# Setting the planned durations of TensorE's and GpSimd's work in a kernel that orders its own instructions

## The chip, the cores and the metric

The kernel runs on one core of a Trainium2 chip. The metric is the device time of one execution in microseconds; lower is better. PE is TensorE, DVE is VectorE, ACT is ScalarE, POOL is GpSimd, and SP is the engine whose queue issues all DMAs here.

## The reference

A decoder trunk of two layers on one sequence of 256 tokens with 1024 features, in float32. Each layer is a token mixer and an MLP, each followed by a LayerNorm of `ALPHA * x + f(x)`:

```python
for i in range(DEPTH):                      # DEPTH = 2
    if i % 2 == 0:
        mix = moba_attention(h, ...)        # 16 heads of 64; one block of 256, so causal attention
    else:
        mix = dilated_attention(h, ...)     # 12 heads: windows (128, 1), (512, 4), (2048, 16)
    h = layer_norm(ALPHA * h + mix, ...)
    h = layer_norm(ALPHA * h + square(relu(h @ w_in)) @ w_out, ...)   # 1024 -> 4096 -> 1024
```

Queries and keys get a rotary embedding. In the second mixer the outputs of the three head groups are weighted by their softmax denominators, which comes to one softmax over the keys of all three groups.

## The kernel before

**Arithmetic.** Each float32 matrix is split into a high and a low part of a shorter format (`split`, L281): ACT writes the high part as a rounded copy, DVE subtracts it from the source for the low part. A product is then three matmuls: high by high, high by low, low by high. A tile of weights is 128 x 1024 (512 KB); it is loaded into one of 4 buffers `raw` and split into `whi` and `wlo`, of which there are 10 each. A `raw` buffer comes free when both splits have read it, a `whi` and `wlo` when PE has used them.

**Steps of PE.** `mm_wstat` (L400) multiplies one tile of weights, held stationary, by all 256 tokens, in eight steps over the features. The narrow form (queries and keys) has three matmuls of 256 columns for a step; the wide form (the MLP's first matrix) has one of 512 and one of 256. `mm_xstat` (L419) holds the tokens stationary; it makes the values ("V steps", n columns each) and the first 512 columns of each MLP. `mm_rows` (L434) adds one tile of a second matrix into the accumulators `acc`, three matmuls for each piece of up to 512 columns ("row steps"). `score` (L500), `transposes` (L534) and `weigh` (L548) are the attention.

**Attention.** For each pair of heads: queries and keys are projected; `rotate` (L464) does three DVE multiplications out of PSUM and one addition on POOL (`ADD_ENG`), and splits the result into `qhi`, `qlo`, `khi`, `klo`, the keys once for each head of the pair. Then come the scores (in PSUM buffers `tp`, of which there are 4), on DVE the mask with the row maximum (`mx`, L515), on ACT the exponentials (L525), on DVE the scaling of `sc` (L532), on PE the transposes, on ACT the copy `pt` to SBUF (L545), and on PE the weighing of the values. Layer 0 has eight such pairs, layer 1 six.

**LayerNorm** (`ln_half`, L618): statistics on DVE, `rstd` as a power on POOL (L638), two DVE steps for each 512 columns, and, but for the last one, transposes and splits into `xs`, the stationary or moving operand of what follows. It is done for the two halves of 128 tokens (m = 0, 1). Behind it the first 512 columns of an MLP go through `hrt` (L699, L700).

**The order of instructions** isn't that of the program text. Each piece of work is given to `plan.op(engine, cost, function, reads, writes)`; `cost` is a planned duration in microseconds, written by hand. `Plan.order` (L112) then simulates the engines with these costs and issues the functions in the order of the planned starts. First a pass in program order gives each PE step a due time, and each other piece the latest time that its users allow:

```python
t = max([clock.get(o.eng, 0.0)] + [p.end + p.lat for p in o.preds])
...
d = q.due - o.cost - o.lat
o.due = d if o.due is None else min(o.due, d)
```

Then a list scheduler takes, engine by engine, the piece that can start first, and of several that can, the one with the earliest due time. A piece can start when its operands are ready (their end plus `LAT` = 0.15 us, none from PE to PE), its engine is free, and its buffers are free. DVE alone may wait for a more urgent piece (`PATIENT`). DMAs keep their program order; a load is planned at 360 GB/s plus 2.1 us. On the chip each engine takes its instructions in the planned order and waits with semaphores for what isn't ready, so whatever stands behind a waiting instruction on that engine waits too. The program order in attention is written out by hand (`ORDER0`, `ORDER1`, L33 to L35).

The planned costs of DVE and ACT are formulas in the number of columns n (L272 to L276): `n / 960 + 0.07` for an ordinary DVE instruction, `n / 1200 + 0.055` for ACT from PSUM and `n / 1200 + 0.093` from SBUF, with additions for scalar operands.

Of the kernel before, what the change touches and what calls it, by code (L numbers as in the profile page):

```python
# [10 lines left out]
ALU = mybir.AluOpType  # L11

P = 128
S = 256
# [49 lines left out]
class Plan:  # L64
# [16 lines left out]
    def op(self, eng, cost, fn, reads=(), writes=(), lat=LAT, early=0.0):  # L81
        o = Op()
        o.n, o.eng, o.cost, o.fn, o.lat = len(self.ops), eng, cost, fn, lat
        o.early = early
        o.preds, o.succs, o.bufs = set(), [], set()
        for group, is_write in ((reads, False), (writes, True)):
            for item in group:
                b, key = item if isinstance(item, tuple) else (item, None)
                o.bufs.add(b)
                for k, st in b.state.items():  # L90
                    if key is None or k is None or k == key:
                        if st[0] is not None:
                            o.preds.add(st[0])
                        if is_write:
                            o.preds.update(st[1])
                st = b.state.setdefault(key, [None, []])
                if is_write:
                    if key is None:
                        b.state = {None: [o, []]}
                    else:  # L100
                        st[0], st[1] = o, []
                else:
                    st[1].append(o)
        o.preds.discard(o)
        for p in o.preds:
            p.succs.append(o)
        for b in o.bufs:
            b.left += 1
        self.ops.append(o)
        return o  # L110
# [112 lines left out]
def tile_trunk(  # L223
# [23 lines left out]
    nc = tc.nc  # L247
    plan = Plan()
    op = plan.op
# [12 lines left out]
    def mk(shape, dt, tag, bufs, space=None):  # L262
        uid[0] += 1
        return plan.buf(Bufs(space or sb, bufs), shape, dt, tag, bufs, f"{tag}_{uid[0]}")
# [80 lines left out]
    expo = mk([P, 1], F32, "expo", 1)  # L345
# [51 lines left out]
    def xk(kt, ms):  # L397
        return [(xs[kt // 4], (part, kt, m)) for part in range(2) for m in ms]

    def mm_wstat(ps, w, kts=range(KT), wide=False):  # L400
        for kt in kts:

            def go(kt=kt):
                c = slice(kt * P, (kt + 1) * P)
                a, b = (xs[kt // 4].t[:, kt % 4, part, :] for part in range(2))
                first, last = kt == 0, kt == KT - 1
                if wide:
                    both = xs[kt // 4].t[:, kt % 4, :, :].rearrange("p h s -> p (h s)")
                    mm(ps.t, w.hi.t[:, c], both, first, False)
                    mm(ps.t[:, S:], w.lo.t[:, c], a, False, last)  # L410
                else:
                    mm(ps.t[:, :S], w.hi.t[:, c], a, first, False)
                    mm(ps.t[:, :S], w.hi.t[:, c], b, False, False)
                    mm(ps.t[:, :S], w.lo.t[:, c], a, False, last)

            i = wkey(w, kt * P)
            op("PE", 0.327, go, [(w.hi, i), (w.lo, i)] + xk(kt, (0, 1)), [ps])

    def mm_xstat(ps, ws, m, n):  # L419
        t = slice(m * P, (m + 1) * P)  # L420
        for kt in range(KT):
            per = 1024 // n
            w = ws[kt // per]

            def go(kt=kt, w=w):
                c = slice((kt % per) * n, (kt % per + 1) * n)
                a, b = (xs[kt // 4].t[:, kt % 4, part, t] for part in range(2))
                mm(ps.t[:, :n], a, w.hi.t[:, c], kt == 0, False)
                mm(ps.t[:, :n], a, w.lo.t[:, c], False, False)
                mm(ps.t[:, :n], b, w.hi.t[:, c], False, kt == KT - 1)  # L430

            op("PE", 3 * (n / 2400 + 0.003), go, [(w.hi, 0), (w.lo, 0)] + xk(kt, (m,)), [ps])

    def mm_rows(pieces, item, m):  # L434
        (ahi, alo, j), w, pos, total = item
        first, last = pos == 0, pos == total - 1
        t = slice(m * P, (m + 1) * P)

        def go():
            a, b = ahi.t[:, j, t], alo.t[:, j, t]  # L440
            for acc, c0, n in pieces:
                mm(acc.t[:, :n], a, w.hi.t[:, c0 : c0 + n], first, False)
                mm(acc.t[:, :n], a, w.lo.t[:, c0 : c0 + n], False, False)
            for acc, c0, n in pieces:
                mm(acc.t[:, :n], b, w.hi.t[:, c0 : c0 + n], False, last)

        op(
            "PE", 3 * sum(n / 2400 + 0.003 for _, _, n in pieces), go,
            [(w.hi, 0), (w.lo, 0), (ahi, (j, m)), (alo, (j, m))], [acc for acc, _, _ in pieces],
        )  # L450

    def tt(n, out_ap, a, b, alu, r, w, eng="DVE"):
        if eng == "DVE":
            op("DVE", dve(n), lambda: nc.vector.tensor_tensor(out_ap(), a(), b(), op=alu), r, w)  # L454
        else:
            op("POOL", n / 480 + 0.1, lambda: nc.gpsimd.tensor_tensor(out_ap(), a(), b(), op=alu), r, w)  # L456

    def stt(n, aps, dst, a, s, b, o0, o1, r, w):
        op(
# [40 lines left out]
    def score(ps, q, k, qc, kc, off=0):  # L500
        (qhi, qlo), (khi, klo) = q, k
        n = kc.stop - kc.start

        def go():
            o = ps.t[:, off : off + 2 * n].rearrange("p (h s) -> p h s", h=2)
            mm(o, qhi.t[:, qc], khi.t[:, :, kc], True, False)
            mm(o, qhi.t[:, qc], klo.t[:, :, kc], False, False)
            mm(o, qlo.t[:, qc], khi.t[:, :, kc], False, True)

        op("PE", 3 * (2 * n / 2400 + 0.003), go, [qhi, qlo, khi, klo], [ps])  # L510

    def mask_min(n, dst, src, mask, init, accum, r, w):
        op(
# [34 lines left out]
    def weigh(o, v, vc, pt, n, c0, start, stop):  # L548
        def go():
            for h in range(2):  # L550
                c = slice(vc + 64 * h, vc + 64 * h + 64)
                mm(o.t[64 * h : 64 * h + 64, c0 : c0 + n], v.t[:, c], pt(h), start, stop)

        return go
# [10 lines left out]
    def pv_causal(p0, p1, r0, r1, v, vc, ahi, alo, j):  # L565
        t0, t1 = psum("tp"), psum("tp")
        transposes(
            t0,
            [(h * S, p0[h]) for h in range(2)] + [(h * S + P, lambda h=h: p1[h]()[:, 0:P]) for h in range(2)],
            r0 + r1,  # L570
        )
        transposes(t1, [(h * P, lambda h=h: p1[h]()[:, P:S]) for h in range(2)], r1)
        pt0, pt1 = copy_out(512, t0, "pt0"), copy_out(S, t1, "pt1")
        o = psum("tp")
        op("PE", 0.482, weigh(o, v[0], vc, lambda h: pt0.t[:, h * S : (h + 1) * S], S, 0, True, False),
           [v[0], pt0], [o])
        op("PE", 0.27, weigh(o, v[1], vc, lambda h: pt1.t[:, h * P : (h + 1) * P], P, P, False, True),
           [v[1], pt1], [o])
        attn_out(o, ahi, alo, j, True)

    def pv_full(e, c0, r, v, vc, ahi, alo, j):
        pts = []
        for kb in range(2):
            t = psum("tp")
            transposes(
                t, [(h * S + m * P, lambda h=h, m=m, kb=kb: e[m][h].t[:, c0 + kb * P : c0 + (kb + 1) * P])
                    for h in range(2) for m in range(2)], r,
            )
            pts.append(copy_out(512, t, f"pt{kb}"))
        o = psum("tp")  # L590
        for kb in range(2):
            op("PE", 0.482,
               weigh(o, v[kb], vc, lambda h, kb=kb: pts[kb].t[:, h * S : (h + 1) * S], S, 0, kb == 0, kb == 1),
               [v[kb], pts[kb]], [o])
        attn_out(o, ahi, alo, j, False)

    def pv_diag(e, c0, r, v, vc, ahi, alo, j):
        t = psum("tp")
        transposes(
            t, [(h * S + m * P, lambda h=h, m=m: e[m][h].t[:, c0 : c0 + P]) for h in range(2) for m in range(2)], r  # L600
        )
        pt = copy_out(512, t, "pt0")
        o = psum("tp")
        for m in range(2):
            op("PE", 0.27,
               weigh(o, v[m], vc, lambda h, m=m: pt.t[:, h * S + m * P : h * S + (m + 1) * P], P, m * P, True, True),
               [v[m], pt], [o])
        attn_out(o, ahi, alo, j, False)
# [9 lines left out]
    def ln_half(pieces, m, gb, last):  # L618
        g, b = gb
# [4 lines left out]
        rs = mk([P, 2], F32, "rstd", 4)  # L624
        prev = []
        ns = D // step
        for acc, c0, n in pieces:
# [7 lines left out]
        op("DVE", 0.08, lambda: nc.vector.bn_aggr(mv.t, st.t[:, :ns, :]), [st], [mv])  # L635
        op("DVE", 0.07, lambda: nc.vector.tensor_scalar(rs.t[:, 0:1], mv.t[:, 1:2], EPS, None, op0=ALU.add),  # L636
           [mv], [(rs, 0)])
        op("POOL", 0.46, lambda: nc.gpsimd.tensor_tensor(rs.t[:, 1:2], rs.t[:, 0:1], expo.t, op=ALU.pow),  # L638
           [(rs, 0), expo], [(rs, 1)])
        for n in range(2):  # L640
            c = slice(n * 512, (n + 1) * 512)
# [11 lines left out]
            if not last:  # L653
                ps = psum("tp")
# [373 lines left out]
```

## Time and profile before

| | |
|---|---|
| median of 3 runs | 583.98 us (583.85 to 585.54) |
| profiled execution | 584.83 us, its span 583.1 us |
| PE busy, of the span | 565.6 us (97%) |
| DVE, ACT, POOL busy | 74%, 51%, 6% |
| matmuls | 3234 |
| TensorE clock granted, mean | 0.996 |
| HBM read | 104.01 MB |

In the profile the span runs from the first to the last instruction. A busy time counts a matmul with its way through the array, so neighbouring matmuls overlap in it; the pace of PE is read from start to start. The time goes through six stages: an opening that waits for the first weights (to 12 us), the attention of layer 0 with its projection and LayerNorm (to about 125 us), its MLP (to about 303 us), the attention of layer 1 (to about 393 us), its MLP (to about 575 us) and the last LayerNorm. L289 is the line of every matmul, L285 that of every low split and L282 of every high one, so the tiles' names tell them apart.

### The profile page before, as it was taken

What the parts mean: (1) busy time and instruction counts of PE and PEld (TensorE: products, weight loads), DVE (VectorE), ACT (ScalarE), POOL (GpSimd) and SP (SyncE); (2) the same over time, 40 slices, a digit from 0 to 9 for tenths busy, and PEclk for the clock granted to TensorE, in tenths of its full rate; (3) what the DMA queues carried; (4) which work ended last, traced back from release to release, by engine and by line L of the source; (5) the groups of instructions that cost most, each with busy time, mean ns of one, the idle gap of its engine ahead of it and who ended that gap; (6) DMA issues with size and microseconds to landing.
All of it is one profiled execution on the core that took longest, in us unless ns stands there. A gap on an engine that the chain in (4) does not pass through costs nothing.

```text
span 583.1 us, 8692 instructions
## 1 busy us (share of the span) xinstructions
PE 565.6 (97%) x3234; PEld 486.0 (83%) x3234; DVE 431.3 (74%) x769; ACT 298.2 (51%) x501; POOL 36.6 (6%) x41
## 2 busy tenths in 40 slices
PE   7999999999999999999999999999999999999994
PEld 6889897788888888888888997987888888888884
DVE  5999989887785665666768799978787656656644
ACT  6567857636654554554533536754674545545400
POOL 0211122010000000000000321000000000000000
PEclk9999999999999999999999999999999999999998
DMA  8894743617877555566523723444878565655101
GB/s 248 279 332 133 234 142 100 209 54 224 293 255 257 190 201 184 184 193 197 187 73 117 279 75 109 144 151 147 282 243 296 183 186 187 198 186 182 37 1 72
DMA packets 31290, 105.62 MB, mean 181 GB/s; under 512 B 3600, under 2 KB 5136, under 8 KB 31248
## 3 DMA queue, kind: packets, MB, share of 16 engines
q1 hardware_dynamic: 31248, 105.07, 54.7%
q8 instruction: 25, 0.41, 0.3%
q14 instruction: 17, 0.14, 0.1%
HBM read 104.01 MB, written 1.05 MB: 180 GB/s over the span
## 4 chain that ended last, share of the span: by engine, by line
PE 79%; DVE 8%; DMA 6%; issue 3%; ACT 2%; POOL 1%; SPq 1%; POOLq 0%; DVEq 0%; ACTq 0%
PE acc L289 41%; PE tp L289 35%; DMA raw<-in_wqk_dram 5%; DVE wlo L285 3%; DVE ta L454 2%; PE tp L537 2%; DMA raw<-in_wv_dram 1%; POOL ta L456 1%; SPq L279 1%; DVE klo L461 1%; ACT whi L282 1%; DVE sc L532 1%; DVE tok L461 0%; DVE sc L515 0%; ACT khi L481 0%
## 5 line engine op out<-in xcount | busy, mean ns | idle before, releaser
L285 DVE TENSOR_TENSOR wlo<-raw,whi 128x1024 fp32r<-128x1024 f32 (+2 forms) x191 | 225.8, 1195 | 95.1 <-ACT whi L282 94.4
L282 ACT ACTIVATE whi<-raw 128x1024 fp32r<-128x1024 f32 (+2 forms) x191 | 194.8, 1026 | 185.4 <-PE tp L289 82.3
L289 PE MATMUL tp<-xs,whi 128*128 128x512 f32 x448 | 159.0, 399 | 0.0
L289 PE MATMUL tp<-xs,wlo 128*128 128x256 f32 x448 | 125.8, 281 | 0.0
L289 PE MATMUL acc<-whi,ahi 128*128 128x512 f32 (+1 forms) x312 | 119.5, 383 | 0.0
L289 PE MATMUL acc<-wlo,ahi 128*128 128x512 f32 (+1 forms) x312 | 117.3, 380 | 0.0
L289 PEld LDWEIGHTS tp<-xs,whi 128*128 128x128 f32 x448 | 84.2, 188 | 20.4
L289 PE MATMUL acc<-whi,alo 128*128 128x512 f32 (+1 forms) x312 | 100.3, 379 | 0.0
L289 PE MATMUL acc<-xs,whi 128*128 128x256 f32 x448 | 84.4, 288 | 2.1 <-ACT whi L282 2.1
L289 PEld LDWEIGHTS tp<-xs,wlo 128*128 128x128 f32 x448 | 84.6, 189 | 0.3
L289 PEld LDWEIGHTS acc<-xs,whi 128*128 128x128 f32 x448 | 70.3, 192 | 5.2 <-ACT whi L282 3.1
L289 PEld LDWEIGHTS acc<-whi,ahi 128*128 128x128 f32 x312 | 58.6, 188 | 11.9 <-issue 0.6
L289 PEld LDWEIGHTS acc<-wlo,ahi 128*128 128x128 f32 x312 | 58.7, 188 | 10.4
L289 PEld LDWEIGHTS acc<-whi,alo 128*128 128x128 f32 x312 | 57.1, 188 | 10.5
L289 PE MATMUL acc<-xs,wlo 128*128 128x256 f32 x224 | 63.7, 284 | 0.2 <-DVE wlo L285 0.2
L289 PEld LDWEIGHTS acc<-xs,wlo 128*128 128x128 f32 x224 | 43.0, 192 | 0.6 <-DVE wlo L285 0.4
L454 DVE TENSOR_TENSOR ta<-acc,ropet 64x256 f32<-64x256 f32 (+1 forms) x84 | 35.1, 420 | 3.4 <-PE acc L289 2.5
L289 PE MATMUL acc<-whi,xs 128*128 128x512 f32 (+1 forms) x128 | 37.3, 366 | 0.3 <-ACT xs L282 0.3
L456 POOL TENSOR_TENSOR ta<-ta,ta 128x256 f32<-128x256 f32 x28 | 28.0, 1003 | 125.5 <-DVE ta L454 122.1
L638 POOL TENSOR_TENSOR rstd<-rstd,expo 128x1 f32<-128x1 f32 x8 | 7.9, 987 | 414.6 <-DVE rstd L636 414.6
L289 PEld LDWEIGHTS acc<-whi,xs 128*128 128x128 f32 x128 | 23.1, 189 | 4.6 <-ACT xs L282 0.5
L454 DVE TENSOR_TENSOR ta<-tp,ta 128x256 f32<-128x256 f32 x56 | 23.5, 419 | 4.6 <-ACT ta L689 4.6
(71 smaller groups left out, 536.2 us busy)
## 6 DMA issues: line engine op xcount, KB each, us to landing
raw<-in_win_dram SPq DMA_DIRECT2D x64, 512.0 KB, 4.3
raw<-in_wout_dram SPq DMA_DIRECT2D x64, 512.0 KB, 4.3
raw<-in_wqk_dram SPq DMA_DIRECT2D x24, 512.0 KB, 4.1
raw<-in_wo_dram SPq DMA_DIRECT2D x14, 512.0 KB, 3.3
raw<-in_wv_dram SPq DMA_DIRECT2D x8, 512.0 KB, 6.6
g<-in_lng_dram SPq DMA_DIRECT2D x4, 512.0 KB, 6.7
b<-in_lnb_dram SPq DMA_DIRECT2D x4, 512.0 KB, 8.2
raw<-in_wv1a_dram SPq DMA_DIRECT2D x4, 512.0 KB, 3.9
```

The costliest lines, as they stand in the source:

```text
L279: op("SP", nbytes / 360e3, lambda: nc.sync.dma_start(dst(), src), reads, writes, lat=2.1)
L282: op("ACT", act(n, sbuf=sbuf), lambda: nc.scalar.activation(hi(), src(), AF.Copy), r, whi)
L285: lambda: nc.vector.tensor_tensor(lo(), src(), f32(hi()), op=ALU.subtract), list(r) + list(whi), wlo,
L289: nc.tensor.matmul(out_ap, lhsT, rhs, start=start, stop=stop)
L454: op("DVE", dve(n), lambda: nc.vector.tensor_tensor(out_ap(), a(), b(), op=alu), r, w)
L456: op("POOL", n / 480 + 0.1, lambda: nc.gpsimd.tensor_tensor(out_ap(), a(), b(), op=alu), r, w)
L461: lambda: nc.vector.scalar_tensor_tensor(dst(), a(), s(), b(), op0=o0, op1=o1), r, w,
L532: op("DVE", dve(n, 1, True), lambda: nc.vector.tensor_scalar(e(), e(), s(), None, op0=ALU.mult), r, w)
L537: nc.tensor.transpose(ps.t[:, c : c + P], src(), ident.t)
L638: op("POOL", 0.46, lambda: nc.gpsimd.tensor_tensor(rs.t[:, 1:2], rs.t[:, 0:1], expo.t, op=ALU.pow), [(rs, 0), expo], [(rs, 1)])
```

## The change

Only the `cost` arguments of PE and POOL pieces are altered; no instruction is added, removed or altered. The planner orders the same pieces by other planned durations, so the order of instructions on all engines can come out differently, that of the DMAs on SP's queue not, though they may be placed otherwise against the rest.

| piece | planned before, us | planned after, us |
|---|---|---|
| `mm_wstat` step, wide / narrow | 0.327 / 0.327 | 0.35 / 0.36 |
| each matmul of n columns in `mm_xstat`, `mm_rows`, `score` | n/2400 + 0.003 | n/2400 + 0.0135 |
| weighing, 256 columns / 128 columns | 0.482 / 0.27 | 0.432 / 0.22 |
| POOL addition of n columns | n/480 + 0.1 | n/480 + 0.15 |
| `rstd` on POOL | 0.46 | 0.98 |

```diff
-            op("PE", 0.327, go, [(w.hi, i), (w.lo, i)] + xk(kt, (0, 1)), [ps])
+            op("PE", 0.35 if wide else 0.36, go, [(w.hi, i), (w.lo, i)] + xk(kt, (0, 1)), [ps])
...
-            op("PE", 3 * (n / 2400 + 0.003), go, [(w.hi, 0), (w.lo, 0)] + xk(kt, (m,)), [ps])
+            op("PE", 3 * (n / 2400 + 0.0135), go, [(w.hi, 0), (w.lo, 0)] + xk(kt, (m,)), [ps])
...
-            "PE", 3 * sum(n / 2400 + 0.003 for _, _, n in pieces), go,
+            "PE", 3 * sum(n / 2400 + 0.0135 for _, _, n in pieces), go,
...
-            op("POOL", n / 480 + 0.1, lambda: nc.gpsimd.tensor_tensor(out_ap(), a(), b(), op=alu), r, w)
+            op("POOL", n / 480 + 0.15, lambda: nc.gpsimd.tensor_tensor(out_ap(), a(), b(), op=alu), r, w)
...
-        op("PE", 3 * (2 * n / 2400 + 0.003), go, [qhi, qlo, khi, klo], [ps])
+        op("PE", 3 * (2 * n / 2400 + 0.0135), go, [qhi, qlo, khi, klo], [ps])
...
-        op("PE", 0.482, weigh(o, v[0], vc, lambda h: pt0.t[:, h * S : (h + 1) * S], S, 0, True, False),
+        op("PE", 0.432, weigh(o, v[0], vc, lambda h: pt0.t[:, h * S : (h + 1) * S], S, 0, True, False),
            [v[0], pt0], [o])
-        op("PE", 0.27, weigh(o, v[1], vc, lambda h: pt1.t[:, h * P : (h + 1) * P], P, P, False, True),
+        op("PE", 0.22, weigh(o, v[1], vc, lambda h: pt1.t[:, h * P : (h + 1) * P], P, P, False, True),
...
-        op("POOL", 0.46, lambda: nc.gpsimd.tensor_tensor(rs.t[:, 1:2], rs.t[:, 0:1], expo.t, op=ALU.pow),
+        op("POOL", 0.98, lambda: nc.gpsimd.tensor_tensor(rs.t[:, 1:2], rs.t[:, 0:1], expo.t, op=ALU.pow),
```

The weighing in the second layer's `pv_full` and `pv_diag` gets the same 0.432 and 0.22.

More of the change, by code (lines that the diff above doesn't have):

```diff
@@ L591, in pv_full @@
         for kb in range(2):
-            op("PE", 0.482,
+            op("PE", 0.432,
                weigh(o, v[kb], vc, lambda h, kb=kb: pts[kb].t[:, h * S : (h + 1) * S], S, 0, kb == 0, kb == 1),
@@ L604, in pv_diag @@
         for m in range(2):
-            op("PE", 0.27,
+            op("PE", 0.22,
                weigh(o, v[m], vc, lambda h, m=m: pt.t[:, h * S + m * P : h * S + (m + 1) * P], P, m * P, True, True),
```

## The prediction

> **What bounds the kernel now.** First the page's head and its busy table, then busy time by stretch, then who waited for whom in front of PE.
>
> ```profile
> span 583.1 us, 8692 instructions
> PE 565.6 (97%) x3234; PEld 486.0 (83%) x3234; DVE 431.3 (74%) x769; ACT 298.2 (51%) x501; POOL 36.6 (6%) x41
> ```
>
> ```profile
> 0.00:12.00 12.00, 8.92 (x42) 7.05 (x42) 5.33 (x14) 6.50 (x13) 0.76 (x5) 1.00 0.75 221
> 12.00:45.00 33.00, 30.95 (x205) 27.74 (x205) 29.91 (x67) 21.85 (x45) 5.48 (x6) 1.00 0.85 300
> 45.00:75.00 30.00, 30.00 (x199) 26.20 (x198) 27.41 (x67) 22.96 (x51) 3.90 (x4) 1.00 0.60 195
> 75.00:90.00 15.00, 13.80 (x114) 12.94 (x113) 13.56 (x35) 8.08 (x15) 3.92 (x4) 1.00 0.42 139
> 90.00:125.00 35.00, 35.00 (x199) 27.83 (x198) 30.55 (x70) 21.56 (x51) 3.42 (x3) 1.00 0.43 136
> 125.00:150.00 25.00, 24.18 (x130) 20.46 (x129) 19.55 (x26) 12.14 (x17) 0.99 (x1) 1.00 0.56 185
> 150.00:303.00 153.00, 153.00 (x760) 129.04 (x759) 102.92 (x148) 73.77 (x110) 0.98 (x1) 1.00 0.62 202
> 303.00:345.00 42.00, 41.41 (x284) 37.91 (x283) 35.73 (x71) 20.62 (x29) 8.22 (x8) 1.00 0.44 151
> 345.00:360.00 15.00, 13.89 (x104) 11.65 (x103) 13.71 (x36) 9.52 (x21) 3.53 (x4) 1.00 0.25 80
> 360.00:416.00 56.00, 55.18 (x336) 47.28 (x335) 48.29 (x86) 31.63 (x51) 3.45 (x4) 1.00 0.51 168
> 416.00:564.20 148.20, 148.20 (x809) 127.95 (x809) 93.52 (x138) 69.62 (x105) 0.00 (x0) 1.00 0.55 181
> 564.20:583.10 18.90, 11.04 (x72) 9.94 (x70) 10.79 (x22) 0.00 (x0) 1.97 (x2) 0.89 0.15 55
> ```
>
> Each row gives a stretch, its length, the busy time of PE, PEld, DVE, ACT and POOL, PE's granted clock, the share of the DMA engines and GB/s. PE is the bound: in the two MLP stretches (150 to 303 and 416 to 564.2) it is busy 153.00 of 153.00 and 148.20 of 148.20 us. All idle time of PE is 583.10 - 565.58 (the page's 565.6) = 17.5 us. Of that 12.00 - 8.92 = 3.1 us lie ahead of the first weights and 18.90 - 11.04 = 7.9 us behind the last matmul, in the last LayerNorm. The remaining 6.6 us lie in between: 2.05 from 12 to 45, 1.20 from 75 to 90, 0.82 from 125 to 150, 0.59 from 303 to 345, 1.11 from 345 to 360, 0.82 from 360 to 416. Since the order of PE's work cannot shorten a matmul, a better order can win part of these 6.6 us, and a worse one has no such limit. By cause:
>
> ```profile
> PE tp L537 <- ACT hrt L700: 1.6, 2, 0.8
> PE tp L537 <- DVE mx L515: 1.2, 1, 1.2
> PE tp L289 <- DVE warm L348: 1.2, 1, 1.2
> PE tp L289 <- ACT pt L545: 1.1, 1, 1.1
> PE acc L289 <- DVE wlo L285: 0.7, 2, 0.5
> PE tp L537 <- DVE sc L532: 0.7, 1, 0.7
> PE tp L289 <- DVE klo L461: 0.6, 2, 0.3
> ```
>
> Four causes lie in the attention stages: mx, pt, sc and klo, together 1.2 + 1.1 + 0.7 + 0.6 = 3.6 us. The two waits for hrt (0.8 each) stand behind a LayerNorm, where all PE work needs its result.
>
> **The change part by part.** Nothing is added or removed; numbers the planner believes are altered. How far was each from the trace?
>
> ```profile
> 150.04 10.90 PE acc L289 x48
> 160.95 11.17 PE tp L289 x63
> ```
>
> ```profile
> 33.77 0.40 PE L289 MATMUL acc<-xs,whi 128*128 128x256 f32 x2
> 34.01 0.28 PE L289 MATMUL acc<-xs,wlo 128*128 128x256 f32 x1
> 34.13 0.28 PE L289 MATMUL acc<-xs,whi 128*128 128x256 f32 x1
> ```
>
> A row step is six matmuls of 512: 10.90 x 6/48 = 1.363 us, where the old plan has 3 x 2 x (0.2133 + 0.003) = 1.298 and the new one 1.361. A wide step is two of 63 matmuls: 0.355 us against 0.327 old and 0.35 new. A narrow step, from 33.77 to 34.13, takes 0.36 us against 0.327 old and 0.36 new. So PE's old figures were 5 to 9% short and the new ones are right. What about the figures left alone?
>
> ```profile
> 21.88 3.49 DVE L285 TENSOR_TENSOR wlo<-raw,whi 128x1024 fp32r<-128x1024 f32 x3
> ```
>
> ```profile
> 30.05 1.04 ACT L282 ACTIVATE whi<-raw 128x1024 fp32r<-128x1024 f32 x1
> 31.00 0.58 ACT L612 ACTIVATE v<-acc 128x512 f32<-128x512 f32 x1
> ```
>
> Three DVE splits in a row take 3.49/3 = 1.16 us each (plan: 1024/960 + 0.07 = 1.137); ACT's split takes 31.00 - 30.05 = 0.95 us from start to start (plan 0.946). These were right before. DMA's are not: the plan moves 360 GB/s, 1.456 us for 512 KB, and from 12 to 45 us, with the DMA engines 85% busy, 300 GB/s came, 1.75 us for 512 KB.
>
> *MLP stages (301 us).* Nothing: PE has no idle time there, and DVE and ACT are busy 67% and 48% (102.92 and 73.77 of 153.00). Those 50 us of free DVE time are the cover; only if a new order used it up would PE wait. I take 0.
>
> *rstd on POOL, 0.46 to 0.98.*
>
> ```profile
> 300.16 0.16 DVE L636 TENSOR_SCALAR rstd<-mv 128x1 f32<-128x1 f32 x1
> 300.23 1.41 DVE L461 SCALAR_TENSOR_TENSOR tok<-tok,mv,g 128x512 f32<-128x512 f32 x2
> ```
>
> ```profile
> L638 POOL TENSOR_TENSOR rstd<-rstd,expo 128x1 f32<-128x1 f32 x8 | 7.9, 987 | 414.6 <-DVE rstd L636 414.6
> ```
>
> The new figure matches the 987 ns. Two DVE steps that don't need rstd take 1.41 us meanwhile (planned 1.33), so it is hidden in either plan; what moves is the due time of the statistics ahead of it, by half a us, before weight splits. 0, and without the cover at most 8 x 0.1 us.
>
> *The opening (12 to 45 us).*
>
> ```profile
> 41.33 1.06 ACT L282 ACTIVATE whi<-raw 128x1024 fp32r<-128x1024 f32 x1 [1.21 <-DMA raw<-in_wqk_dram]
> 42.29 0.85 ACT L545 ACTIVATE pt<-tp 128x512 f32<-128x512 f32 x2
> ```
>
> Here ACT's order was planned for data that came later than planned. It stood 1.21 us before a weight split whose DMA hadn't landed; behind that split were queued the copies pt, and PE stood 1.1 us for them (row pt above). Slowing the planned PE while leaving the planned DMA fast pulls the two apart further. Some 17 us of this stretch are narrow steps, planned 9% too short, and 14 us are V steps and scores, planned 5% too short: the planned PE moves back by about 1.5 + 0.7 = 2.2 us by the end of it. By that much more the plan believes that weights lead, which is two ACT splits of 0.95. Each split that goes ahead of a copy or a key head can stop ACT as at 41.33. Bounds: -1.1 (the one stop goes away) to +2.2 (all the added lead becomes waiting). I take one more stop, +1.1, nearest to the row at 41.33.
>
> *Attention, from a projection to its score.*
>
> ```profile
> 77.92 1.28 DVE L454 TENSOR_TENSOR ta<-acc,ropet 128x256 f32<-128x256 f32 x3
> 79.23 1.23 DVE L285 TENSOR_TENSOR wlo<-raw,whi 128x1024 fp32r<-128x1024 f32 x1
> ```
>
> ```profile
> 81.63 0.89 DVE L461 SCALAR_TENSOR_TENSOR klo<-ta,hm,khi 128x256 fp32r<-128x256 f32 x2 [1.17 <-ACT khi L481]
> ```
>
> ```profile
> 79.34 1.71 POOL L456 TENSOR_TENSOR ta<-ta,ta 128x256 f32<-128x256 f32 x1 [2.49 <-DVE ta L454]
> ```
>
> ```profile
> L456 POOL TENSOR_TENSOR ta<-ta,ta x28: 724/742/1720, 17.7 to 366.7; 128x256 f32<-128x256 f32 x28
> ```
>
> From the first rotation to the second klo the new plan has 3 x 0.337 + POOL 0.683 + two khi of 0.399 + klo 0.397, with three hand-overs of 0.15: 3.34 us (old 3.29). The trace has 77.92 to 81.63 + 0.89, 4.6 us, of which POOL's add is 1.71. Of all 28 adds the median is 742 ns and the longest 1720. The new 0.683 fits the median and not the long ones, which coincide with a DVE split. The planner puts narrow steps on PE until the score is ready. With 3.3 us plus two hand-overs, 3.59/0.327 = 11 steps before and 3.64/0.36 = 10.1 now: on average nearly one step, 0.32 us of real work, less. The old plan bought 0.3 us of margin with its error; the new one has none left for a late add. One step less counts only where PE already arrives first: two klo waits in the trace. Bounds -0.6 (both waits go) to 14 scores x 0.36 = 5.0; I take two steps of 0.36, +0.7.
>
> The Trainium skill ("SBUF — State Buffer", section "Who interferes with whom") says that a DVE instruction with two SBUF inputs and a GpSimd instruction that reads SBUF exclude one another for a whole instruction, which speaks against a fixed POOL figure. The row of 1.71 us beside a split that began 0.11 us earlier agrees. Without that rule every add would take 0.742, the chain 3.6 us, and this term of the sum would be about half, +0.35.
>
> *Attention, from a score to its transposes.* The waits for mx (1.2) and sc (0.7) are of this kind: PE reaches the transposes before DVE has freed the scores' PSUM or scaled them. Their DVE and ACT figures were right, so here too the cover shrinks by about one step where PE waits already: 2 x 0.36 = +0.7, between -1.9 (both go) and 14 x 0.36 = 5.0. The pairs transposes to weighing are planned 0.05 us shorter per instruction and stay behind ACT's copy: 0.
>
> *The tail.* 7.9 us of LayerNorm and output in an order fixed by dependencies: 0, at most half a us either way for a moved DVE step of 0.7.
>
> Sum: 1.1 + 0.7 + 0.7 = +2.5 us. The profiled execution took 584.83 us, 1.7 beyond its span and 0.85 above the median of the three runs, 583.98. On it the sum gives 587.3; against the median, 586.5. That is +0.43%; a measurement of this kernel can tell about 0.3%, 1.75 us, from no change.
>
> **The rivals.** *Faster: the order fits the real pace.* With PE's true durations the planner sees which operand is late and puts other work there. For it: PE's figures were the only wrong ones among the three compute engines, and four of the seven waits above, in the attention stages, hang on what the planner put where. Price: the attention waits, 3.6 us, go: 583.98 - 3.6 = 580.4; with the two wlo waits of the opening 0.7 more, 579.7. It decides if at least half of the 3.6 us goes and no stop like that of 41.33 comes new. Against it: the same rows show DMA and POOL still planned short.
>
> *No change beyond 0.3%: the order moves where it costs nothing.* For it: from 45 to 75 and 90 to 125 us PE is busy 30.00 of 30.00 and 35.00 of 35.00 even in attention, so most steps may swap without a wait. That the altered figures move almost no instruction falls here too. 584.0.
>
> *Much slower: DVE becomes the bound in attention.* DVE is busy 29.91 of 33.00, 13.56 of 15.00 and 13.71 of 15.00 us, 91%. Head-of-line stops that take over 9% of such a stretch reach PE fully; one more ACT stop of 1.2 us in each of the eight pairs of layer 0 would give about 9 us, 593.
>
> **How the numbers follow.** Forecast (slower by lost margin, 585.7 to 590) 0.38; much slower 0.08; faster 0.31; within 0.3% 0.23. The predicted time is that of the forecast, 586.5, whose own range is 585.7 to 590. The range to hold 8 in 10 runs from 580.0, which takes in most of the faster case, to 591.0. Chances: faster 0.31, same 0.23, slower 0.46.
>
> **What would show it.** Right: from 12 to 45 us PE's idle time grows from 2.05 to about 3 us, with ACT waiting longer for wqk or wv; the waits of PE for klo, mx or sc from 345 to 360 or 75 to 90 grow; the MLP stretches stay full and the tail is 7.9 us. Wrong: PE idle between 12 and 564 us falls below 5 us (the faster rival), or MLP stretches show PE waits, or the start or the tail carries the difference.

## The result and the profile after

The changed kernel takes 591.35 us (median; 590.58 to 592.12) against 583.91 us for the kernel before: slower by 7.4 us, a ratio of 1.0128 with a 95% interval of 1.0113 to 1.0143. The profiled execution took 592.12 us, its span 589.9 us, 6.8 more than before.

The page's head, its busy table and the row of POOL's additions, of after:

```profile
span 589.9 us, 8696 instructions
PE 568.8 (96%) x3234; PEld 487.9 (83%) x3234; DVE 430.8 (73%) x769; ACT 299.3 (51%) x501; POOL 39.5 (7%) x41
...
L456 POOL TENSOR_TENSOR ta<-ta,ta 128x256 f32<-128x256 f32 x28 | 30.8, 1105 | 129.3 <-DVE ta L454 120.4
```

The work is the same, 3234 matmuls. PE's idle time grew from 17.5 to 589.9 - 568.8 = 21.1 us, and its busy time by 3.2 us. Of the busy time, the clock, below, explains 1.7. A part of the rest is how busy time is counted: a matmul counts with its way through the array, so a gap looks shorter than the time that it costs (the three gaps near 355 us, below, cost 2.8 us from start to start, and 2.2 of it are counted as idle). The stretches that answer to those of before (PE's busy time is the third number, its clock the third from the end):

```profile
12.00:45.00 33.00, 30.44 (x202) 27.07 (x201) 29.32 (x65) 21.54 (x44) 6.31 (x6) 1.00 0.83 297
45.00:75.00 30.00, 28.63 (x187) 24.77 (x187) 29.28 (x68) 22.09 (x49) 4.84 (x4) 1.00 0.65 204
75.00:90.00 15.00, 14.11 (x116) 13.24 (x114) 13.61 (x28) 10.38 (x20) 3.46 (x3) 1.00 0.54 188
90.00:125.00 35.00, 34.08 (x201) 28.03 (x202) 29.30 (x74) 17.96 (x47) 3.20 (x4) 1.00 0.36 121
125.00:150.00 25.00, 23.68 (x123) 19.73 (x122) 21.98 (x30) 15.95 (x24) 0.98 (x1) 1.00 0.61 193
150.00:303.00 153.00, 153.00 (x764) 129.19 (x763) 97.92 (x141) 71.86 (x106) 0.00 (x0) 1.00 0.61 197
...
345.00:360.00 15.00, 12.65 (x85) 10.66 (x84) 13.41 (x40) 8.44 (x18) 3.91 (x4) 0.96 0.23 75
360.00:416.00 56.00, 55.05 (x338) 45.86 (x336) 48.92 (x93) 31.44 (x53) 5.30 (x5) 0.98 0.49 152
```

The first MLP is as full as before. Stretches in which PE was never idle, 45 to 75 and 90 to 125 us, now have 1.4 and 0.9 us of idle time; from 345 to 360 it is 2.35 us where it was 1.11. From 12 to 560 us PE's idle time grew from 6.6 to 11.7 us, by 5.1; the start, up to 12 us, was 1.0 us better in this execution (2.1 us idle, 3.1 before). By PE's own timeline, the same piece of work begins later by this much:

| PE begins | before | after | later by |
|---|---|---|---|
| LayerNorm transposes after layer 0's attention | 121.9 | 123.8 | 1.9 |
| the same after the first MLP | 303.0 | 305.6 | 2.6 |
| first score of layer 1 | 330.1 | 333.2 | 3.1 |
| V steps of 256 columns in layer 1 | 365.4 | 371.6 | 6.2 |
| LayerNorm transposes after layer 1's attention | 390.5 | 397.2 | 6.7 |
| end | 583.1 | 589.9 | 6.8 |

Who PE waited for, after:

```profile
PE tp L289 <- ACT pt L545: 2.9, 3, 2.3
PE tp L537 <- ACT hrt L700: 2.7, 4, 0.8
PE tp L289 <- DVE mx L515: 1.6, 1, 1.6
PE tp L289 <- DVE warm L348: 1.2, 1, 1.2
PE tp L537 <- DVE sc L532: 1.0, 1, 1.0
PE tp L537 <- DVE mx L515: 1.0, 1, 1.0
PE acc L289 <- ACT whi L282: 0.8, 1, 0.8
PE tp L289 <- DVE klo L461: 0.6, 1, 0.6
PE tp L289 <- ACT khi L481: 0.6, 1, 0.6
PE acc L289 <- DVE xs L285: 0.5, 1, 0.5
```

Waits for pt went from 1.1 to 2.9, for mx from 1.2 to 2.6, for hrt from 1.6 to 2.7, for khi and klo from 0.6 to 1.2, for sc from 0.7 to 1.0. Waits for weights at the start fell; in before they were the longest row:

```profile
PE acc L289 <- ACT whi L282: 2.1, 2, 1.9
```

No single wait makes the loss; it is spread over the joints between a chain on ACT and DVE and the PE work that uses it. By kind and place, eight joints after 12 us have a wait where before had none. Seven of them (PE's timeline, after):

```profile
51.75 0.41 PE L537 MATMUL tp<-ident,sc 128*128 128x128 f32 x2 [0.97 <-DVE mx L515]
67.25 0.87 PE L289 MATMUL tp<-pt,v 128*64 128x256 f32 x8 [0.40 <-ACT pt L545]
81.53 0.87 PE L289 MATMUL tp<-pt,v 128*64 128x256 f32 x8 [0.21 <-ACT pt L545]
90.92 0.87 PE L289 MATMUL tp<-pt,v 128*64 128x256 f32 x8 [1.61 <-DVE mx L515]
143.17 0.66 PE L537 MATMUL tp<-ident,hrt 128*128 128x128 f32 x4 [0.50 <-ACT hrt L700]
316.55 0.72 PE L289 MATMUL acc<-whi,xs 128*128 128x512 f32 x2 [0.46 <-DVE xs L285]
416.64 0.66 PE L537 MATMUL tp<-ident,hrt 128*128 128x128 f32 x4 [0.60 <-ACT hrt L700]
```

With the wait for khi at 354.81, below, they cost 5.3 us. Three waits that before had too grew, by 1.8 us together (pt near 42 us, klo and sc near 355 us), and four waits of before, 2.2 us together, are gone. In layer 1 three waits follow one another (PE's timeline, after):

```profile
353.94 0.28 PE L289 MATMUL acc<-xs,wlo 128*128 128x256 f32 x1
354.81 0.50 PE L289 MATMUL tp<-khi,qhi 128*128 128x512 f32 x1 [0.59 <-ACT khi L481]
355.91 0.50 PE L289 MATMUL tp<-klo,qhi 128*128 128x512 f32 x1 [0.60 <-DVE klo L461]
...
358.38 0.76 PE L537 MATMUL tp<-ident,sc 128*128 128x128 f32 x2 [1.02 <-DVE sc L532]
```

and PE's clock falls behind them (stretches of 3 us, after):

```profile
354.00:357.00 3.00, 1.81 (x8) 1.06 (x7) 2.97 (x6) 3.00 (x9) 0.00 (x0) 1.00 0.32 79
357.00:360.00 3.00, 1.97 (x8) 1.01 (x7) 2.92 (x8) 2.31 (x4) 0.72 (x1) 0.79 0.24 96
360.00:363.00 3.00, 3.00 (x16) 1.99 (x16) 2.96 (x9) 2.09 (x4) 0.90 (x1) 0.64 0.02 5
363.00:366.00 3.00, 3.00 (x28) 2.31 (x28) 2.25 (x4) 1.18 (x3) 0.00 (x0) 1.00 0.55 175
```

At 0.79 and 0.64 of the clock, 3 x 0.21 + 3 x 0.36 = 1.7 us of PE work are lost, all counted as busy. In before the clock was whole from 345 to 360. This fall is not what makes the loss: two of the four executions of after have a mean clock of 0.995 and took 591.8 and 592.1 us, the other two have 0.998, a loss of under 1.5 us over the whole span and so less than this fall, and still took 590.6 and 590.9, 6.7 us or more above before.

### The profile page after: what moved, and what is told of

Same layout as the page of the kernel before. It is cut to its first block, busy times and chain, and to the rows that moved or that the text cites. A ratio compares the mean times of both kernels' runs of the same rounds, so it can differ in the third digit from the quotient of the medians.

```text
span 589.9 us, 8696 instructions
## 1 busy us (share of the span) xinstructions
PE 568.8 (96%) x3234; PEld 487.9 (83%) x3234; DVE 430.8 (73%) x769; ACT 299.3 (51%) x501; POOL 39.5 (7%) x41
## 4 chain that ended last, share of the span: by engine, by line
PE 68%; DVE 18%; DMA 5%; issue 3%; ACT 2%; POOL 2%; SPq 1%; DVEq 0%; POOLq 0%; ACTq 0%
PE acc L289 37%; PE tp L289 30%; DVE wlo L285 5%; DVE ta L454 4%; DVE tok L461 3%; DMA raw<-in_wqk_dram 3%; POOL ta L456 2%; DMA raw<-in_win_dram 1%; PE tp L537 1%; SPq L279 1%; DVE klo L461 1%; DVE xs L285 1%; DVE bst L632 1%; DMA raw<-in_wv_dram 1%; DVE sc L515 1%
## 5 line engine op out<-in xcount | busy, mean ns | idle before, releaser
L456 POOL TENSOR_TENSOR ta<-ta,ta 128x256 f32<-128x256 f32 x28 | 30.8, 1105 | 129.3 <-DVE ta L454 120.4
```

The lines of the kernel that those rows point to most:

```text
L456: op("POOL", n / 480 + 0.15, lambda: nc.gpsimd.tensor_tensor(out_ap(), a(), b(), op=alu), r, w)
```

## The experiments

The theory to test is the forecast's: PE's old figures were too short, the planner therefore put more PE work beside each chain than it believed, and the true figures take that cover away. Its rivals: POOL's figures, the planned DMA rate, the exclusion between POOL's additions and DVE's splits, and mere chance, that any other order of this kernel lands some us off. Times are medians; each ratio is to the kernel before on the same chip, with its 95% interval.

**Which figures.** One run has the change without the two POOL figures, one has these alone.

> The change without its two POOL figures (addition and rstd as before); PE's figures as after. Lost margin on PE: all of the loss stays, 590 to 592 us, with PE's waits for khi, klo and sc near 354 us. POOL's own figures at fault: 584 to 585. Chance (any other order of this kernel lands some us off, before is a lucky one): anything from 584 to 593, and stages that don't match those of after.

> Only the two POOL figures changed (addition 0.683, rstd 0.98); PE's as before. Lost margin: 583.5 to 585, no change. POOL's figures at fault: 590 or more. Chance: a change of one to several us in either direction, since some 2 to 3 per cent of DVE's and ACT's instructions change places.

591.55 us, 1.0142 (1.0125 to 1.0158), and 583.28 us, 0.9994 (0.9985 to 1.0004). PE's figures make the whole loss, POOL's none. PE's figures include those of weighing, which the change shortens; no run has them alone.

**How much of them.** PE's figures half way, and moved on by another half. The figures of weighing move with them the other way (0.457 and 0.407 for 256 columns), and POOL's are those of after:

```diff
-            op("PE", 0.35 if wide else 0.36, go, ...
+            op("PE", 0.3385 if wide else 0.3435, go, ...      # half; 0.3615 and 0.3765 moved on
...
-            op("PE", 3 * (n / 2400 + 0.0135), go, ...
+            op("PE", 3 * (n / 2400 + 0.00825), go, ...        # half; 0.01875 moved on
```

> After, with PE's figures half way between before's and after's (POOL's as after). Lost margin: the loss grows with PE's planned time, so about half of it, 586 to 588.5. Chance: anything from 582 to 592, not between the two.

> After, with PE's figures moved on by another half of the change (narrow step 0.3765, wide 0.3615, overhead of a matmul 0.01875), some 3% longer than measured. Lost margin: more loss than after, 593 to 596, with longer waits for khi, klo and sc in layer 1. Chance: 582 to 592. If true figures are the worst by accident of the order alone: better than after.

587.53 us, 1.0091 (1.0060 to 1.0122), and 598.58 us, 1.0259 (1.0232 to 1.0286). Half of the change makes about half of the loss; beyond the true figures it goes on, faster than in proportion. The clock has a part in the last: in that profile it was granted at 0.97, 0.95 and 0.95 from 12 to 45, 45 to 75 and 90 to 125 us, some 4 us of PE work, and was whole there in after. The same step in the other direction (wide 0.3155 and narrow 0.3105, overhead -0.00225, weighing 0.507):

> PE's figures moved from before's by half the change in the other direction (narrow step 0.3105, wide 0.3155), POOL's as after. Cover theory: no further loss; a little faster if waits of before (3.6 us in attention) still lacked cover, 581 to 583.5, else the same. Chance: 582 to 592. If before's figures were an optimum: 585 to 588.

580.66 us, 0.9942 (0.9925 to 0.9960): faster than before. One row for each profile shows how the loss builds up: the stretch from 12 to 560 us, with PE's busy time and its number of matmuls. With PE's figures shortened, of before, half way, of after, moved on:

```profile
12.00:560.00 548.00, 544.88 (x3125) 468.94 (x3124) 415.41 (x733) 291.51 (x488) 34.62 (x34) 1.00 0.56 186
```

```profile
12.00:560.00 548.00, 541.41 (x3104) 465.55 (x3104) 414.97 (x733) 291.75 (x489) 33.88 (x34) 1.00 0.56 186
```

```profile
12.00:560.00 548.00, 538.75 (x3093) 463.53 (x3092) 412.97 (x731) 290.62 (x488) 35.87 (x34) 1.00 0.57 186
```

```profile
12.00:560.00 548.00, 536.27 (x3070) 460.26 (x3069) 411.81 (x728) 291.40 (x486) 36.74 (x34) 1.00 0.56 186
```

```profile
12.00:560.00 548.00, 533.66 (x3041) 457.88 (x3040) 409.12 (x720) 288.98 (x481) 35.99 (x34) 0.99 0.56 186
```

Five planned lengths of PE, five orders, and in that sequence PE is idle 3.1, 6.6, 9.3, 11.7 and 14.3 us and gets 3125, 3104, 3093, 3070 and 3041 matmuls done. The medians keep to the same sequence. Five orders that had nothing to do with PE's figures would fall into it in one of 120 cases.

The orders themselves, as each kernel's `Plan.order` gives them, let the cover be counted: the PE work, at the true lengths, that stands between the last PE step that a chain starts from and the PE step that uses the chain. From a score to its transposes (24 chains) it is 11.6 us on average in before and 10.9 in after, less in 16 of the 24; against before it is +0.65 us with the shortened figures, -0.69 half way, -0.70 in after and -1.03 moved on. From a projection to its score (28 chains) it is 7.9 us in before and in after, and the same in 26 of the 28. For the transposes of `hrt` nothing changed. So cover in PE steps was lost behind the scores. At the other joints the same PE steps stand ahead, and the chain itself ends later. The order changed more on ACT and DVE, where 15% and 12% of the pieces stand elsewhere than in before, than on PE, where 4% do; that this is the reason is shown for the waits for hrt, below, and not for the others.

**Which PE steps.** The steps of the projections and the MLP's first matrix alone, and the overhead of V steps, row steps and scores alone:

> Only the figures of the projection and first-matrix steps changed (0.327 to 0.36 and 0.35); all others as before. Lost margin: these steps are the cover of the rotations, so most of the loss, 587 to 590. Chance: 582 to 592, and not adding up with the next kernel to the whole loss of 7.4.

> Only the overhead of a matmul in V steps, row steps and scores changed (0.003 to 0.0135); all others as before. Lost margin: these steps are seldom the cover of a chain in attention, so 584 to 587, the part of the loss that the projections don't have. Chance: 582 to 592, not adding up with the kernel before it to 7.4.

589.62 us, 1.0098 (1.0072 to 1.0124), and 587.90 us, 1.0070 (1.0051 to 1.0088). The projections have the larger part, but the two differences, 6.0 and 4.3 us, add up to more than the whole 7.4. The second was expected smaller. So beside the trend a single order has some us of its own.

**Is it the ratio to the chains?** After, with nearly everything that PE's work covers planned 7% longer:

```diff
-        return n / 960 + ...                       # DVE; ACT and POOL's addition likewise
+        return 1.07 * (n / 960 + ...)
-LAT = 0.15
+LAT = 0.1605
```

> After (PE's figures true), and the planned durations of DVE, ACT and POOL's addition and the hand-over LAT all 7% longer, which gives the chains the same ratio to PE as in before. Cover theory (what counts is how long a chain is planned beside the PE work that covers it): back to before, 583 to 585.5. If longer PE figures are bad by themselves: 589 to 592.

584.58 us, 1.0013 (1.0000 to 1.0025). With PE's true figures kept, 6.8 of the 7.4 us are back. What counts is the planned chain against the planned cover, not PE's figure by itself. That order is close to before's, as it must be when nearly everything is planned longer by a like part: by the planner's lists 4% of DVE's pieces stand elsewhere, against 12% in after. So this run tells a ratio to the chains from a ratio to the DMAs, which weren't made longer, but not by which joints the time comes back. The cluster of waits for khi, klo and sc stands in it too (0.6, 0.6 and 0.7 us from 350 to 354 us), with a whole clock behind it.

**The DMA rate.** After and before with `nbytes / 300e3` in place of `nbytes / 360e3`, and before with 382e3, which gives DMA the lead over PE that the change gave it:

> After, and DMAs planned at 300 GB/s, the rate of the opening, instead of 360. DMA theory (ACT's order in the opening counts on weights that come later): the wait of PE for pt at 40 to 43 us falls from 2.3 us to under 0.5, and 1 to 2 us are won, 589 to 590; layer 1's attention stays as after. Lost margin alone: 591. Chance: 584 to 593, with the attention of layer 1 changed too.

> Before, with DMAs planned at 300 GB/s. Lead theory: the wait of PE for pt near 42 us goes (1.1 us) and the attention of layer 0 ends 1 to 2 us earlier; layer 1 as before if its order holds, 581.5 to 583. Chance: 582 to 590.

> Before, with DMAs planned at 382 GB/s instead of 360: PE's planned durations stay short, but DMA gets the lead over PE that the change gave it (PE's planned sum grew by 6%). Lead theory (what counts is the ratio of planned PE to planned DMA): the wait of PE for pt near 42 us grows from 1.1 to 2 us or more and the attention of layer 0 ends 1 to 3 us later, 585 to 588. If PE's figures count by themselves: 583.5.

586.08 us, 1.0051 (1.0034 to 1.0069); 580.68 us, 0.9945 (0.9926 to 0.9964); 583.90 us, 0.9999 (0.9981 to 1.0017). A planned rate nearer to that of the opening wins 5.3 us on after and 2.9 on before, more than I expected of either. In after with 300 GB/s PE's wait for pt near 42 us is gone and the waits for hrt are back at 1.6 us. The loss is for the most part not the DMA figure's: at 300 GB/s in both, PE's new figures still cost 586.08 - 580.68 = 5.4 us. And the lead theory fails its own test: at 382 GB/s the order costs nothing, and PE's waits for pt in the whole run shrink instead of growing (before 1.1 in one):

```profile
PE tp L289 <- ACT pt L545: 1.0, 2, 0.8
```

the larger of these at 365 us; the one at 41 us is 0.2. All that is left of PE's waits in before with 300 GB/s is the start and what stands behind a LayerNorm:

```profile
PE tp L537 <- ACT hrt L700: 1.6, 2, 0.8
PE acc L289 <- ACT whi L282: 1.3, 1, 1.3
PE tp L289 <- DVE warm L348: 1.2, 1, 1.2
PE acc L289 <- ACT xs L282: 0.3, 1, 0.3
```

Does it add to the other reserves?

> As e13, and DMAs planned at 300 GB/s. If the reserve of the chains and the true DMA rate act separately: about 3 us under e13, 580 to 582, as e7. If DMA's figure only acted through chance: 582 to 588.

> As e14, and DMAs planned at 300 GB/s. More cover than e7: 579 to 581.5 if cover still lacks somewhere, the same as e7 (580.7) if e7 has all that is to be had but for the two waits behind the LayerNorms.

583.62 us, 1.0001 (0.9987 to 1.0015): 1.0 under the same without it, not 3, which lies in the range that was named for chance. It is no clean test: beside PE and chains that are planned 6 to 7% longer, 300 GB/s is like 300 x 1.07 = 321 beside those of before. And 580.01 us, 0.9934 (0.9909 to 0.9960), the lowest median of all, though not apart from 580.66 and 580.68 by these intervals. All three versions with less than 581 us beat before and after. A shorter planned PE and a slower planned DMA don't add: with either alone most attention waits are gone.

**Is a stage's loss its own?** The new figures in layer 1 alone:

> The change's figures for the work of layer 1 alone (its attention and MLP); layer 0 planned as before. If the losses of the stages are separate, layer 0 and the way into layer 1 run as before and the cluster of waits with the half clock comes back: plus 3 to 5 us, 587 to 589, PE idle near 350 to 355 us. If the loss in layer 1 only follows from a different state left by layer 0: 583 to 585.

586.19 us, 1.0047 (1.0027 to 1.0068), 2.6 us slower, just under the range. The cluster of waits for khi, klo and sc came back at 351 to 355 us, and the half clock behind it, while PE reached layer 1's first score at 329.1 us, 1.0 earlier than in before. Layer 1's loss doesn't need that of layer 0.

**Additions behind splits.** After, with the planner told that a POOL addition and a split between SBUF tiles don't run together:

```diff
             s = max(o.ready, free[o.eng])
+            if o.port:                                  # set for additions on POOL and splits from SBUF
+                s = max(s, port["POOL" if o.eng == "DVE" else "DVE"])
```

> After, and the planner is told that a POOL addition and a DVE split with both inputs in SBUF exclude each other: each is planned to start after the other's end. Port theory (the new order puts 10 additions behind splits, 1.7 us instead of 0.74, where before had 7; the plan doesn't see it and queues qlo ahead of the next rotation): the waits of DVE for qhi (5.8 us) shrink to about 2, the cluster near 354 us goes, 586 to 588. Lost margin: as after, 590 to 592. Chance: no relation to the number of long additions.

589.74 us, 1.0116 (1.0081 to 1.0150), within the interval of after's ratio. The cluster near 354 us went but a wait of 2.3 us for klo came at 335 us, and additions still start beside splits. But there are fewer: 10 of over 1.6 us in after, 7 with this edit, 7 in before. With no more long additions than before had, most of the loss stays (6.2 us), so their number isn't its cause; that one of them delays a chain here and there isn't excluded.

**The clock.** After with work in the gap:

```diff
         def go():
+            for _ in range(warmers):                    # 10 for the first transposes of layer 1, else 0
+                mm(ps.t[:, :P], ident.t, ident.t, True, True)
             for c, src in pairs:
```

> After, with ten matmuls of the identity by itself ahead of the first transposes of layer 1, where PE stands idle for about 1.2 us anyway; their result is overwritten by the transposes, and the planned costs are untouched, so the order stays. Clock theory (in after, PE's clock is granted at half from 359 to 363 us, behind a cluster of waits, and that costs about 1.8 us): with the gap filled the clock stays whole and the time falls by 1.5 to 2 us, to 589.5 to 590. If the waits alone cost the time: 591.3, or up to 1 us more.

591.18 us, 1.0124 (1.0084 to 1.0164): no gain. In its profile the clock did stay whole at that place, but it fell at another, where after had it whole (the two kernels' stretch from 88 to 96 us; first after, then with the fill):

```profile
88.00:96.00 8.00, 6.39 (x55) 5.95 (x54) 7.19 (x23) 6.01 (x16) 0.72 (x1) 1.00 0.38 122
```

```profile
357.00:360.00 3.00, 2.69 (x19) 2.50 (x20) 2.91 (x8) 2.75 (x7) 0.73 (x1) 1.00 0.51 180
360.00:363.00 3.00, 3.00 (x26) 2.48 (x25) 2.94 (x10) 2.03 (x3) 0.83 (x1) 1.00 0.00 0
...
88.00:96.00 8.00, 6.12 (x40) 5.69 (x39) 6.34 (x21) 5.34 (x16) 0.72 (x1) 0.79 0.38 122
```

The order of instructions in both is the same, and PE is idle about as long there (1.6 and 1.9 us). So the fill keeps the clock whole where it stands, but which cluster of waits pays differs between executions, and the time that the fill is worth stays open.

## Why the prediction was right or wrong

**Right:** the direction, and the cause: true PE figures beside unchanged chains make the order worse. The series of five PE lengths, and the 7% longer chains that give the time back, show it. Where the time is lost the forecast had wrong. Steps put at nothing stayed there: the MLP (153.00 of 153.00), rstd and POOL's addition (583.28 with both alone), and the last LayerNorm (25.70 - 18.41 = 7.3 us idle behind 564.2, 7.9 before). Of the signs named in advance, the waits for klo and sc from 345 to 360 us grew (0.29 to 0.60 and 0.68 to 1.02), that for mx from 75 to 90 us did not: it is gone, and others for mx stand at 51.8 and 90.9 us. Idle time from 12 to 45 us grew, to 2.56, not 3, and ACT's stop for wqk from 1.21 to 1.84 us.

**Wrong:** the size, +2.5 us against +7.4, above the top of the range, 591.0, by 0.35 us. Of the 6.8 us between the profiled spans, 5.1 are PE's idle time from 12 to 560 us and 3.2 its busy time; the start and the tail gave 1.6 back. Term by term:

*Attention, from a score to its transposes (+0.7)* and *from a projection to its score (+0.7).* I counted lost cover only where PE already waited, two joints of each kind. In sum the waits for mx and sc grew by 1.7 us, those for khi and klo by 0.6. What failed is the rule "counts only where PE already arrives first": with the planned PE some 6% longer, joints with no wait in before got one. The eight of them cost 5.3 us, while at the old joints the waits fell a little in sum (1.8 us more at three, 2.2 less at four). PE was never idle from 45 to 75 and 90 to 125 us, and I took that for slack; it was cover that just sufficed. The step "on average nearly one step less" from a projection to its score failed too: by the orders these PE steps are the same for 26 of 28 scores, and that their term came out near (+0.6 against +0.7) was luck. Cover was lost between the scores and their transposes, 0.7 us on average.

*The opening (+1.1).* The one wait grew as priced, and by one more split ahead of pt, as the text said (ACT's timeline, after):

```profile
39.66 1.06 ACT L282 ACTIVATE whi<-raw 128x1024 fp32r<-128x1024 f32 x1 [1.84 <-DMA raw<-in_wqk_dram]
40.62 0.40 ACT L282 ACTIVATE qhi<-ta 128x256 fp32r<-128x256 f32 x1
40.93 1.04 ACT L282 ACTIVATE whi<-raw 128x1024 fp32r<-128x1024 f32 x1
41.88 0.85 ACT L545 ACTIVATE pt<-tp 128x512 f32<-128x512 f32 x2
```

PE stood 2.3 us for it, 1.2 more than before. But the reason given, that DMA's planned lead over PE does this, didn't hold: 382 GB/s beside the old PE figures made the wait smaller. And the size agrees in part by luck: with PE's figures alone PE waited only 0.7 us there, and the loss was the same; with the fill, in the order of after, it was 1.7. The run with 300 GB/s shows that a slower planned DMA takes this wait away.

*The waits for hrt, taken as fixed.* They went from 1.6 to 2.7 us. The two of 0.82 us, behind a LayerNorm, are unchanged; two new ones, for the second half, cost 0.50 and 0.60. The PE work ahead of them is the same. ACT came late: its order now has a weight split, whose DMA hadn't landed, ahead of hrt (ACT's timeline, after; in before ACT took hrt's first step as soon as PE had it ready, and the split next to it did not wait):

```profile
140.91 1.06 ACT L282 ACTIVATE whi<-raw 128x1024 fp32r<-128x1024 f32 x1 [1.14 <-DMA raw<-in_win_dram]
141.88 0.58 ACT L699 ACTIVATE hrt<-tp 128x512 f32<-128x512 f32 x1
```

At 414.37 us the same stop is 1.43 us long. It is the stop that I had priced for the opening and had not looked for behind a LayerNorm.

*The clock, not in the sum at all*: 1.7 us in the profiled execution, not in all. I treated waits as adding one for one; in this execution a cluster of 2.2 us of them was followed by the loss of 1.7 more.

**The rivals.** Of the faster rival's two premises the runs turn one around: the planner, told PE's true pace, did not put work where an operand is late, since it still doesn't know of what makes operands late. Its price was nearly right for another edit, a shorter planned PE: 580.66 against the 580.4 worked out, and of the 3.6 us of waits only one for sc, 0.4, is left. "No change" holds for POOL's figures alone. "Much slower" named a further stop of 1.2 us in each pair of layer 0; there are three waits for pt in all, one of them that long.

## What to carry to other kernels

In a list scheduler whose order is fixed ahead, the planned durations are also the only reserve. If chains end later on the chip than planned (here late DMAs that hold up ACT's queue are the best shown reason: planned at 300 GB/s they give 5.3 us back), then a figure that is too short for the covering engine hides it, and correcting that figure alone takes the reserve away. Joints at which nothing waits are no proof of slack. So correct the durations of a plan together, or correct one and add the lost reserve to the chains by intent (7% here); and test a planned figure in steps to both sides before settling on the measured one.

## What the runs showed of the hardware

PE's clock fell to half although no wait was long. In after, 353.9 to 358.4 us has three gaps, the longest 358.38 - 356.96 less one matmul of 0.23, about 1.2 us; then half the clock, and back:

```profile
360.00:361.00 1.00, 1.00 (x6) 1.00 (x5) 0.95 (x4) 0.74 (x2) 0.23 (x1) 0.50 0.00 0
```

It is 0.50 from 359 to 362 us, 0.74 in the half us before and 0.85 in the half us behind: 3.4 us in all (1.7 us lost at half rate). The Trainium skill ("TensorE: Matmul & The Clock Gate", section "Part 1: The HAM clock gate") describes a free-running window of about 3.4 us after which the clock is halved or restored; the length agrees, and that the place changes between executions of one order is in line with it. The Trainium skill's rule of no idle gaps of more than about 3.4 us (same page, section "HAM oscillation") does not cover this case: the fall came behind gaps of 0.8 to 1.2 us close together, with PE busy 3.8 of the 6 us from 354 to 360.
